# Retention outputs stored from POOL's queue, and adaLN products ordered behind a tile's decayed scores on VectorE

## The chip, the core and the metric

The kernel runs on one core of a Trainium2 chip. A core has TensorE (matrix products), VectorE, ScalarE, GpSimd (POOL) and SyncE (SP, which here only starts transfers), each with an instruction stream of its own that it takes in order, and 16 DMA engines. The metric is the device time of one launch in microseconds. Three runs of the kernel before gave 1794.5, 1806.36 and 1819.52 us, median 1806.36.

## What is computed

One layer of a diffusion backbone over 1024 tokens of width 1024, with 256 context tokens, all in float32: adaLN-modulated RMSNorm, one input projection split into differential attention and bidirectional retention, gates, output projection, then a mixture of 64 experts. The part that matters here is the retention output, and the adaLN vectors that are computed beside it:

```python
mod_x = jax.nn.silu(c) @ ada_w[l] + ada_b[l]
...
scores = jnp.einsum('bnihd,bnjhd->bnhij', qc, kc) * decay
intra = jnp.einsum('bnhij,bnjhe->bnihe', scores, vc)
...
cross = jnp.einsum('bnihd,nbhde->bnihe', q_dec, state_prev)
out = (intra + cross).reshape(b, t, h, dv)
...
r = jax.nn.silu(gate) * rmsnorm(ret, ret_norm_g).reshape(bn, t, R_V)
```

The forward and the backward direction are added; the kernel takes one two-sided decay matrix and both states stacked.

## The kernel before

The tokens are eight tiles of 128. The kernel goes in stages: adaLN columns and norm, then projections of the retention queries and keys, of the values with the chunk states (lines 503 to 534, ten tiles with the context), then the **retention loop** (lines 566 to 592), then the attention projections, attention, output projection, routing and experts.

The retention loop runs over t = 7 down to 0. In one iteration it transposes the queries and keys of the tile (line 392, `transpose4`), copies them (571, 574), calls `ret_out` for the tile before it, steps the backward state (`state_step`, lines 499 and 500), loads queries, keys and values of the next tile (`load_qkv`, lines 544 and 545, and the decayed queries, 547), projects the gate (24 matmuls of line 228), applies SiLU (582) and multiplies by the norm's weight on POOL (583, the gate product), computes the scores in PSUM (587) and multiplies them by the decay into sT (589, VectorE). `ret_out` multiplies sT with the values and the queries with the state (554, 555), squares the result with its sum (559), takes the reciprocal root (157 on VectorE, 159 a power on POOL), scales and gates it into r_o (563, four operations on VectorE) and stores r_o to `mix_d` in device memory (564, from SP's queue). What is stored there is read again by the output projection (line 874).

The remaining four adaLN vectors are 4096 columns, taken as 64 **products**: for each of 8 blocks of 512 columns and each of 8 slices of the input, 256 KB of weights are loaded (408, SP's queue, two buffers `ada_l`) and multiplied by a scalar per partition into an accumulator of 512 columns (410 for the first slice, 412 for the others, VectorE). `ada_rest(count)` emits `count` of them: three in each of the ten value tiles, and six (`GADA`) in each iteration of the retention loop, called behind sT, till none is left. After the third slice of a block `ada_row` closes the block before it: a matmul with ones sums over partitions (420), a bias row is added (424), and the row is stored.

Within an engine the order of instructions is not the order of the program text: a scheduler sets it when the program is built, by what is ready first in its own estimate, unless an order is asked for. A dependency of the kind NoSync between two instructions of one engine asks for that order and adds no semaphore.

Of the kernel before, what the change touches and what calls it, by code (L numbers as in the profile page):

```python
# [15 lines left out]
OP = mybir.AluOpType  # L16
# [4 lines left out]
P = 128  # L21
# [63 lines left out]
def hybrid_layer_kernel(ctx: ExitStack, tc: tile.TileContext, A, out, dbg=None):  # L85
    nc = tc.nc
    pe, dve, act, pool, sp = nc.tensor, nc.vector, nc.scalar, nc.gpsimd, nc.sync
# [58 lines left out]
    mix_d = dram.tile([SEQ, D], F32, name="mix_d")  # L146
# [7 lines left out]
    def rstd_cols(pl, ssq, n, width, scale):  # L154

        v = pl.tile([P, 8], F32, name="rs_v", tag="rs_v", bufs=4)
        dve.tensor_scalar(v[:n, :width], ssq, scale, EPS, op0=OP.mult, op1=OP.add)  # L157
        r = pl.tile([P, 8], F32, name="rs_r", tag="rs_r", bufs=4)
        pool.tensor_tensor(r[:n, :width], v[:n, :width], mhalf[:n].to_broadcast([n, width]), op=OP.pow)  # L159
        return r[:n, :width]  # L160
# [64 lines left out]
    def project(t, w, n0=0, n1=512):  # L225
        ps = psa.tile([P, 512], F32, name="pp", tag="pp", bufs=2)
        for kw in products(ps, t, w, n0, n1):
            pe.matmul(kw["out"], kw["lhsT"], kw["rhs"], start=kw["start"], stop=kw["stop"])  # L228
        return ps
# [28 lines left out]
    cc = consts.tile([P, KT, 2], F32, name="cc")  # L258
# [21 lines left out]
    for kind in range(2):  # L280
        for fb in range(2):
            dve.tensor_scalar(Wd[:, kind, :, fb], lg[:, 4 * fb:4 * fb + 4], pw[:, 2 * kind + fb:2 * kind + fb + 1],
                              None, op0=OP.mult)
# [105 lines left out]
    def transpose4(src, tag):  # L389
        pt = psa.tile([P, 4, P], F32, name="p4", tag=tag, bufs=2)  # L390
        for i in range(4):
            pe.transpose(pt[:, i, :], src[:, i * P:(i + 1) * P], ident)
        return pt
# [3 lines left out]
    VADA, GADA = 3, 6  # L397
    ada_acc = {}
    ada_left = [(n, k) for n in range(8) for k in range(KT)]

    def ada_rest(count):

        for n, k in ada_left[:count]:
            if k == 0:
                ada_acc[n] = wk.tile([P, 512], F32, name="ada_a", tag="ada_a", bufs=2)
            ac = ada_acc[n]
            aw = wk.tile([P, 512], F32, name="ada_l", tag="ada_l", bufs=2)
            sp.dma_start(aw, ada[:, k, 2048 + 512 * n:2560 + 512 * n])
            if k == 0:
                dve.tensor_scalar(ac, aw, cc[:, 0, 0:1], None, op0=OP.mult)  # L410
            else:
                dve.scalar_tensor_tensor(ac, aw, cc[:, k, 0:1], ac, op0=OP.mult, op1=OP.add)
            if k == 2 and n > 0:
                ada_row(n - 1)
        del ada_left[:count]

    def ada_row(n):
        c0 = 2048 + 512 * n
        pr_ = psa.tile([1, 512], F32, name="par", tag="po", bufs=2)
        pe.matmul(pr_, ones[:, 0:1], ada_acc.pop(n), start=True, stop=True)  # L420
        rw = wk.tile([1, 512], F32, name="ada_r", tag="ada_r")
        bw = wk.tile([1, 512], F32, name="ada_b", tag="ada_b")
        sp.dma_start(bw, A["ada_b"][:, c0:c0 + 512])
        dve.tensor_add(rw, pr_, bw)
        if n // 2 == 2:
            gw = wk.tile([1, 512], F32, name="ada_g", tag="ada_b")
            sp.dma_start(gw, A["norm2_g"][:, (n % 2) * 512:(n % 2 + 1) * 512])
            dve.scalar_tensor_tensor(rw, rw, 1.0, gw, op0=OP.add, op1=OP.mult)
        sp.dma_start(rows_d[n // 2:n // 2 + 1, (n % 2) * 512:(n % 2 + 1) * 512], rw)
# [15 lines left out]
    for i, g in enumerate(pairs):  # L445
        for t in (2 * g - 2, 2 * g - 1):
            if t < 0:
                ps = project(t, W, 256, 512)
                r = wk.tile([P, 256], F32, name="rkc", tag="rkc", bufs=2)
# [14 lines left out]
    Dm = wk.tile([P, H, P], F32, name="Dm")  # L464
# [31 lines left out]
    def state_step(dst, src, kvp, half):  # L496
        s = slice(64 * half, 64 * half + 64)
        tmp = wk.tile([P, H, P], F32, name="sst", tag="g2", bufs=NG2)
        dve.tensor_tensor(tmp[s], src[s], GSb[s], op=OP.mult)
        dve.tensor_add(dst[s], tmp[s], kvp[s])  # L500

    kvc0 = None
    for t in range(-2, NT):
        ada_rest(VADA)
        ps = project(t, W)
        v = wk.tile([P, 512], F32, name="rv", tag="g2", bufs=NG2)
# [35 lines left out]
    def load_qkv(t):  # L542
        qk, vt = rows_qv[:, t % 2, 0], rows_qv[:, t % 2, 1]
        sp.dma_start(qk, rqk_d[t * P:(t + 1) * P])
        sp.dma_start(vt, rv_d[t * P:(t + 1) * P])
        qd = wk.tile([P, H, 2, 64], F32, name="qd", tag="g2", bufs=NG2)
        dve.tensor_tensor(qd, qk[:, 0:256].rearrange("p (h d) -> p h d", h=H)[:, :, None, :].to_broadcast([P, H, 2, 64]),
                          Wd[:, 0, :, :, None].to_broadcast([P, H, 2, 64]), op=OP.mult)
        return qk, vt, qd

    def ret_out(t, sT, qdT, vt, gt):
        po_ = psa.tile([P, H, P], F32, name="po", tag="po", bufs=2)
        for h in range(H):
            pe.matmul(po_[:, h, :], sT[:, 2 * (h % 2) + h // 2, :], vt[:, h * P:(h + 1) * P], start=True, stop=False)
            pe.matmul(po_[:, h, :], qdT[:, h, :], ST[t][:, h, :], start=False, stop=True)
        ssq = wk.tile([P, 4], F32, name="ssq4", tag="ssq4", bufs=2)
        sqs = wk.tile([P, P], F32, name="sqs", tag="sqs", bufs=2)
        for h in range(H):
            act.activation(sqs, po_[:, h, :], AF.Square, accum_out=ssq[:, h:h + 1])
        rs = rstd_cols(wk, ssq, P, 4, 1.0 / P)  # L560
        r = wk.tile([P, H, P], F32, name="r_o", tag="g2", bufs=NG2)
        for h in range(H):
            dve.scalar_tensor_tensor(r[:, h, :], po_[:, h, :], rs[:, h:h + 1], gt[:, h, :], op0=OP.mult, op1=OP.mult)
        sp.dma_start(mix_d[t * P:(t + 1) * P, 512:1024], r.rearrange("p h e -> p (h e)"))

    nxt, out_args = load_qkv(NT - 1), None
    for t in reversed(range(NT)):
        qk, vt, qd = nxt
        pt = transpose4(qk, "tp")
        qkT = wk.tile([P, 4, P], F32, name="qkT", tag="g2", bufs=NG2)  # L570
        act.activation(qkT, pt, AF.Copy)
        pt = transpose4(qd.rearrange("p h a d -> p (h a d)"), "tp")
        qdT = wk.tile([P, H, P], F32, name="qdT", tag="g2", bufs=NG2)
        act.activation(qdT, pt, AF.Copy)
        if out_args:
            ret_out(*out_args)
        if t > 0:
            state_step(ST[t - 1], ST[t], ST[t - 1], 1)
            nxt = load_qkv(t - 1)
        ps = project(t, W)  # L580
        gt = wk.tile([P, H, P], F32, name="gt", tag="g2", bufs=NG2)
        act.activation(gt.rearrange("p h e -> p (h e)"), ps, AF.Silu)
        pool.tensor_tensor(gt, gt, rng[:, None, :].to_broadcast([P, H, P]), op=OP.mult)
        pss = psa.tile([P, 2, 4, P], F32, name="pss", tag="ps", bufs=1)
        for h in range(H):
            s = slice(64 * (h % 2), 64 * (h % 2) + 64)
            pe.matmul(pss[:, h % 2, h // 2, :], qkT[s, 2 + h // 2, :], qkT[s, h // 2, :], start=True, stop=True)
        sT = wk.tile([P, H, P], F32, name="sT", tag="g2", bufs=NG2)
        dve.tensor_tensor(sT.rearrange("p (a b) j -> p a b j", a=2), pss[:, :, 0:2, :], Dm.rearrange("p (a b) j -> p a b j", a=2), op=OP.mult)
        out_args = t, sT, qdT, vt, gt  # L590
        ada_rest(GADA)
    ret_out(*out_args)
    ada_row(NT - 1)

# [10 lines left out]
    for t in range(NT):  # L605
# [3 lines left out]
        for m in range(2):  # L609
            a, b = slice(64 * m, 64 * m + 64), slice(64 * (1 - m), 64 * (1 - m) + 64)  # L610
            act.activation(qs[a, m], pt[a], AF.Copy, scale=0.125)
            act.activation(qs[b, m], pt[a], AF.Copy, scale=0.125)
            for c in (a, b):
                dve.scalar_tensor_tensor(qs[c, 2 + m], pt[a], 0.125, qs[a, m].bitcast(F32), op0=OP.mult,
                                         op1=OP.subtract)
# [15 lines left out]
    for t in range(-2, NT):  # L631
# [8 lines left out]
        for m in range(2):  # L640
            a, b = slice(64 * m, 64 * m + 64), slice(64 * (1 - m), 64 * (1 - m) + 64)
# [662 lines left out]
    rest, order, lead = list(range(NEXP)), [], 0.0  # L1304
    while rest:
        r = rest.pop(0 if lead <= 0 else -1)
# [186 lines left out]
    with tc.For_i(0, n_over, 1) as j:  # L1493
        e = sp.value_load(olist[0:1, 0, bass.ds(j, 1)], min_val=0, max_val=NEXP - 1)
# [14 lines left out]
        for q in range(2):  # L1509
            pt = bank("tr", [P, 4, P])  # L1510
            for i in range(4):
                k = 4 * q + i
# [72 lines left out]
```

## Time and profile before

| what | us |
|---|---|
| median of three runs | 1806.36 |
| lowest, highest | 1794.5, 1819.52 |
| the profiled execution | 1810.34 |
| its span (first to last instruction) | 1808.5 |
| TensorE, VectorE, ScalarE, POOL busy | 1661.3, 1354.5, 960.8, 539.9 |

The profile is of one execution. It gives for each instruction its start, its length, its source line, and for idle time of an engine the event that ended it. In a name such as `ada_a<-ada_l,cc,ada_a` the output stands first and the inputs behind the arrow. PEld is TensorE's weight load, which overlaps the matmuls; SPq and POOLq are the instructions of those queues that start transfers. PEclk is the granted TensorE clock as a share of the full one. Matmuls are pipelined and their ends are modelled.

### The profile page before, as it was taken

How to read it: one execution, taken by the hardware profiler on the slowest of the kernel's cores; microseconds unless marked ns; L12 is line 12 of the kernel's file. 1: busy time of each engine (PE TensorE's matmuls, PEld its weight loads, DVE VectorE, ACT ScalarE, POOL GpSimd, SP SyncE). 2: the span in 40 equal slices, each digit the busy share in tenths (PEclk: the TensorE clock that was granted, in tenths of full speed). 3: DMA queues.
4: the chain of work that ended last, by engine and by line, in shares of the span. 5: the costliest groups of instructions: out<-in, count | busy, mean ns of one | idle time of the engine just before them, and what ended most of it. 6: DMA issues, size and time to landing. Idle time of an engine off the chain costs nothing.

```text
span 1808.5 us, 23059 instructions
## 1 busy us (share of the span) xinstructions
PE 1661.3 (92%) x8022; PEld 1264.4 (70%) x8022; DVE 1354.5 (75%) x2080; ACT 960.8 (53%) x1537; POOL 539.9 (30%) x384
## 2 busy tenths in 40 slices
PE   5899889999899989886999999999999999999992
PEld 3687677778566657665777777777776777777771
DVE  7866766642877757775678888888888988878873
ACT  6532333323577842131366686677675665566652
POOL 0100123200222130447335544333445333332331
PEclk9999999999899999998999999999999999999996
DMA  9675547601221154233989999999999999999976
GB/s 315 206 225 183 183 129 155 141 0 59 71 70 36 32 195 152 82 119 62 303 245 316 318 331 322 321 311 295 336 322 306 353 332 353 319 293 321 315 221 212
DMA packets 128413, 400.57 MB, mean 221 GB/s; under 512 B 13110, under 2 KB 49654, under 8 KB 103336
## 3 DMA queue, kind: packets, MB, share of 16 engines
q1 hardware_dynamic: 81000, 297.10, 45.8%
q0 software_dynamic: 46144, 97.80, 23.0%
q10 hardware_dynamic: 1152, 4.19, 0.6%
q8 instruction: 64, 1.05, 0.2%
q14 instruction: 53, 0.43, 0.1%
HBM read 324.45 MB, written 74.60 MB: 221 GB/s over the span
## 4 chain that ended last, share of the span: by engine, by line
PE 50%; DMA 18%; DVE 17%; ACT 7%; issue 5%; POOL 1%; SPq 1%; another core or an unknown queue 1%; POOLq 0%; DVEq 0%; ACTq 0%
PE up L1239 16%; DMA acc<-y,sidx 12%; PE py L1239 8%; PE pp L228 7%; PE py L97 3%; DVE w L1169 3%; PE pp L97 3%; PE tr L1223 3%; PE pS L97 3%; PE pu L97 2%; ACT w L1168 2%; DVE nmx L738 2%; DMA eraw<-in_exp_w_dram 1%; DMA ada_l<-in_ada_w_dram 1%; PE ptt L97 1%
## 5 line engine op out<-in xcount | busy, mean ns | idle before, releaser
L1239 PE MATMUL up<-w,xT 128*128 128x512 f32 (+1 forms) x2136 | 531.2, 398 | 6.4 <-DVE xT L1228 6.1
L1169 DVE TENSOR_TENSOR w<-eraw,w 128x1024 fp32r<-128x1024 f32 x390 | 459.7, 1217 | 44.1 <-ACT w L1168 43.3
L1168 ACT ACTIVATE w<-eraw 128x1024 fp32r<-128x1024 f32 x390 | 399.8, 1056 | 114.3 <-PE up L1239 60.7
L1239 PEld LDWEIGHTS up<-w,xT 128*128 128x128 f32 (+1 forms) x2136 | 382.7, 183 | 103.9 <-DVE xT L1228 10.2
L1178 POOL DMA_INDIRECT acc<-y,sidx x96 | 215.2, 2242 | 484.8 <-DMA acc<-y,sidx 158.9
L1239 PE MATMUL py<-w,ehT 128*128 128x512 f32 (+1 forms) x1116 | 293.4, 405 | 4.0 <-DVE ehT L1228 4.0
L1239 PEld LDWEIGHTS py<-w,ehT 128*128 128x128 f32 (+1 forms) x1116 | 198.2, 185 | 51.9 <-DVE ehT L1228 5.3
L1290 DVE SCALAR_TENSOR_TENSOR y<-py,swt,g2r 128x512 f32<-128x512 f32 (+2 forms) x192 | 137.8, 740 | 61.7 <-DMA acc<-y,sidx 39.0
L228 PE MATMUL pp<-whi,hTh 128*128 128x512 f32 (+1 forms) x368 | 146.5, 399 | 1.3 <-ACT hTh L386 1.2
L228 PE MATMUL pp<-wlo,hTh 128*128 128x512 f32 (+1 forms) x368 | 144.7, 394 | 0.0
L738 DVE TENSOR_REDUCE nmx<-pS 128x1 f32<-128x1280 f32 x64 | 95.1, 1487 | 65.8 <-PE pS L97 65.4
L1207 POOL DMA_INDIRECT xg<-h2tab,sidx x96 | 122.3, 1274 | 64.2 <-PE tr L1223 40.6
L1265 ACT ACTIVATE sl<-up 128x256 f32<-128x256 f32 (+1 forms) x104 | 39.7, 382 | 148.4 <-PE up L1239 136.4
L1228 DVE TENSOR_TENSOR xT<-tr,xT 128x512 fp32r<-128x512 f32 (+1 forms) x167 | 104.3, 654 | 17.0 <-ACT xT L1227 13.9
L1027 POOL DMA_INDIRECT slots<-dat,ad x64 | 68.7, 1073 | 109.8 <-DVE dat L1024 54.9
L159 POOL TENSOR_TENSOR rs_r<-rs_v,mhalf 128x1 f32<-128x1 f32 (+1 forms) x34 | 27.3, 802 | 244.3 <-DVE rs_v L157 146.8
L97 PE MATMUL pS<-K,qsl 128*128 128x512 f32 x336 | 95.7, 422 | 2.8 <-ACT an L746 1.9
L1227 ACT ACTIVATE xT<-tr 128x512 fp32r<-128x512 f32 (+1 forms) x167 | 89.1, 571 | 13.0 <-remote 4.4
L1223 PEld LDWEIGHTS tr<-cst,xg 128*128 128x128 f32 (+2 forms) x800 | 79.0, 140 | 22.3 <-issue 7.1
L1267 DVE TENSOR_TENSOR hn<-up,sl 128x256 f32<-128x256 f32 (+1 forms) x104 | 64.8, 623 | 39.3 <-ACT sl L1265 37.0
L97 PE MATMUL py<-wo,mT 128*128 128x512 f32 x384 | 90.7, 394 | 0.0
L1223 PE MATMUL tr<-cst,xg 128*128 128x128 f32 (+2 forms) x800 | 90.3, 253 | 0.1
(324 smaller groups left out, 2490.5 us busy)
## 6 DMA issues: line engine op xcount, KB each, us to landing
eraw<-in_exp_w_dram SPq DMA_DIRECT2D x192, 1024.0 KB
ada_l<-in_ada_w_dram SPq DMA_DIRECT2D x64, 256.0 KB
wraw<-in_w_in_dram SPq DMA_DIRECT2D x24, 512.0 KB
aw<-in_ada_w_dram SPq DMA_DIRECT2D x8, 1024.0 KB
qsp<-qs POOLq DMA_DIRECT2D x32, 256.0 KB
qsl<-qsp POOLq DMA_DIRECT2D x7, 1024.0 KB
xt<-in_x_dram SPq DMA_DIRECT2D x8, 512.0 KB
wor<-in_w_out_dram SPq DMA_DIRECT2D x8, 512.0 KB
```

The lines of the kernel that those rows point to most:

```text
L97: i = getattr(self.eng, name)(*args, **kw)
L228: pe.matmul(kw["out"], kw["lhsT"], kw["rhs"], start=kw["start"], stop=kw["stop"])
L738: dve.tensor_reduce(self.nmx, self.pS, axis=AX.X, op=OP.max, negate=True)
L1168: act.activation(hi, raw, AF.Copy)
L1169: dve.tensor_sub(lo, raw, hi.bitcast(F32))
L1178: x = pool.indirect_dma_start(out=acc, out_offset=bass.IndirectOffsetOnAxis(ap=idx, axis=0), in_=y, in_offset=None, compute_op=OP.add)
L1207: self.load = pool.indirect_dma_start(out=self.xg[:self.n], out_offset=None, in_=h2tab, in_offset=bass.IndirectOffsetOnAxis(ap=self.idx, a ...
L1223: pe.transpose(pt[:, i, :], src[:rows, k * P:(k + 1) * P], ident[:rows, :rows])
L1227: act.activation(hi, pt, AF.Copy)
L1228: dve.tensor_sub(lo, pt, hi.bitcast(F32))
L1239: pe.matmul(po, ops[o][:, k, :], w(k), start=(k == 0 and j == 0), stop=(k == nk - 1 and j == len(seq) - 1))
L1290: dve.scalar_tensor_tensor(y[:n, c], ps[i][:n], self.wt, g2r[:n, c], op0=OP.mult, op1=OP.mult)
```

## The change

The store of r_o is issued by POOL instead of SP. `ada_rest` gets an optional instruction `after`; when it is given, each product gets a NoSync dependency on it, so that it stands behind it in VectorE's order. The retention loop passes the instruction that writes sT. The loads of the products, the row sums and the calls in the value stage are as before.

```diff
@@ -398,7 +398,7 @@
-    def ada_rest(count):
+    def ada_rest(count, after=None):
@@ -407,9 +407,12 @@
             if k == 0:
-                dve.tensor_scalar(ac, aw, cc[:, 0, 0:1], None, op0=OP.mult)
+                x = dve.tensor_scalar(ac, aw, cc[:, 0, 0:1], None, op0=OP.mult)
             else:
-                dve.scalar_tensor_tensor(ac, aw, cc[:, k, 0:1], ac, op0=OP.mult, op1=OP.add)
+                x = dve.scalar_tensor_tensor(ac, aw, cc[:, k, 0:1], ac, op0=OP.mult, op1=OP.add)
+            if after is not None:
+                tc.add_manual_dep(x.ins, after.ins.name, mybir.DependencyInfo(
+                    mybir.DependencyClass.NoSync, mybir.DependencyReason.DATA), reason="issue order")
@@ -561,7 +564,7 @@
-        sp.dma_start(mix_d[t * P:(t + 1) * P, 512:1024], r.rearrange("p h e -> p (h e)"))
+        pool.dma_start(mix_d[t * P:(t + 1) * P, 512:1024], r.rearrange("p h e -> p (h e)"))
@@ -586,9 +589,9 @@
-        dve.tensor_tensor(sT.rearrange("p (a b) j -> p a b j", a=2), pss[:, :, 0:2, :], Dm.rearrange("p (a b) j -> p a b j", a=2), op=OP.mult)
+        decayed = dve.tensor_tensor(sT.rearrange("p (a b) j -> p a b j", a=2), pss[:, :, 0:2, :], Dm.rearrange("p (a b) j -> p a b j", a=2), op=OP.mult)
         out_args = t, sT, qdT, vt, gt
-        ada_rest(GADA)
+        ada_rest(GADA, decayed)
```

## Rows read from the trace of the kernel before

**Rows 1.** The page of the execution: its first line

```profile
span 1808.5 us, 23059 instructions
```

**Rows 2.** Busy time of each engine (instructions), granted clock, DMA share, GB/s, by stretch

```profile
core 0: us, PE busy (x) PEld busy (x) DVE busy (x) ACT busy (x) POOL busy (x), PEclk, DMA share, GB/s
188.50:201.00 12.50, 9.31 (x56) 7.59 (x56) 8.34 (x16) 3.29 (x12) 2.29 (x2) 1.00 0.55 178
201.00:213.50 12.50, 11.85 (x58) 9.12 (x58) 7.89 (x14) 2.44 (x10) 2.31 (x2) 0.86 0.51 159
...
225.40:238.10 12.70, 11.17 (x53) 8.76 (x54) 8.79 (x16) 2.07 (x9) 2.76 (x2) 0.87 0.47 150
...
250.70:259.80 9.10, 8.34 (x51) 6.94 (x52) 5.58 (x12) 2.07 (x9) 1.45 (x2) 1.00 0.37 116
```

**Rows 3.** Waits of 185 to 275 us: who for whom, us in total, times, longest

```profile
PEld po L554 <- DVE sT L589: 12.8, 8, 3.3
...
DVE ada_a L412 <- DMA ada_l<-in_ada_w_dram: 12.0, 11, 2.8
...
SPq L564 <- DVE r_o L563: 21.7, 7, 8.8
```

**Rows 4.** VectorE in order of time: start, us, line, operation [idle before, ended by]

```profile
200.91 0.69 DVE L589 TENSOR_TENSOR sT<-pss,Dm 128x512 f32<-128x512 f32 x1
203.08 0.75 DVE L412 SCALAR_TENSOR_TENSOR ada_a<-ada_l,cc,ada_a 128x512 f32<-128x512 f32 x1 [1.48 <-DMA ada_l<-in_ada_w_dram]
204.72 0.75 DVE L412 SCALAR_TENSOR_TENSOR ada_a<-ada_l,cc,ada_a 128x512 f32<-128x512 f32 x1 [0.89 <-DMA ada_l<-in_ada_w_dram]
206.36 0.17 DVE L157 TENSOR_SCALAR rs_v<-ssq 128x4 f32<-128x4 f32 x1 [0.89 <-ACT sqs L559]
207.72 1.13 DVE L563 SCALAR_TENSOR_TENSOR r_o<-po,rs_r,gt 128x128 f32<-128x128 f32 x4 [1.19 <-POOL rs_r L159]
...
210.32 0.69 DVE L500 TENSOR_TENSOR ST<-sst,ST 64x512 f32<-64x512 f32 x1
211.04 2.43 DVE L412 SCALAR_TENSOR_TENSOR ada_a<-ada_l,cc,ada_a 128x512 f32<-128x512 f32 x2
213.39 0.68 DVE L589 TENSOR_TENSOR sT<-pss,Dm 128x512 f32<-128x512 f32 x1
```

**Rows 5.** TensorE and POOL in order of time, same columns

```profile
210.84 0.71 PE L587 MATMUL pss<-qkT 64*128 64x128 f32 x8
211.48 1.02 PE L420 MATMUL par<-ada_a,ones 128*1 128x512 f32 x2
...
211.62 1.30 POOL L583 TENSOR_TENSOR gt<-gt,rng 128x512 f32<-128x512 f32 x1 [3.93 <-ACT gt L582]
...
259.36 1.57 POOL L583 TENSOR_TENSOR gt<-gt,rng 128x512 f32<-128x512 f32 x1 [2.89 <-ACT gt L582]
```

**Rows 6.** Groups by line, 187 to 275 us: busy us, mean ns, idle before

```profile
L412 DVE SCALAR_TENSOR_TENSOR ada_a<-ada_l,cc,ada_a 128x512 f32<-128x512 f32 x22 | 19.3, 879 | 12.4 <-DMA ada_l<-in_ada_w_dram 12.0
...
L410 DVE TENSOR_SCALAR ada_a<-ada_l,cc 128x512 f32<-128x512 f32 x3 | 2.4, 816 | 0.0
```

**Rows 7.** Chain of waits in order of time: start, us, what (slow and full clock)

```profile
203.01 0.43 PE po L554 x2
...
252.17 0.22 PE po L554 x2
```

**Rows 8.** Busy time by stretch, columns as in rows 2, behind the loop

```profile
275.00:300.00 25.00, 25.00 (x114) 19.98 (x113) 15.81 (x30) 6.92 (x12) 6.98 (x9) 1.00 0.56 111
```

**Rows 9.** Instructions of lines 589 and 617: ns min/median/max, first and last start

```profile
L589 DVE TENSOR_TENSOR sT<-pss,Dm x8: 678/684/693, 188.5 to 270.1; 128x512 f32<-128x512 f32 x8
...
L617 POOL DMA_DIRECT2D qsp<-qs x32: 708/892/1057, 287.8 to 339.0; - x32
```

**Rows 10.** SP's queue in order of time

```profile
208.87 0.33 SPq L564 DMA_DIRECT2D mix_d<-r_o  x1
211.82 0.33 SPq L408 DMA_DIRECT2D ada_l<-in_ada_w_dram  x1
```

## Prediction, written before the changed kernel was run

> **What bounds the kernel now.** I read the page first: the span is 1808.5 us [rows 1]; the execution profiled took 1810.3 us, 1.8 us around its span and 4 us above the median of the three runs, 1806.4. The change touches one stage, the retention loop (lines 567 to 592, eight tiles from t = 7 down to 0). I found its place by the decayed scores sT, one per tile: they start at 188.5, 201, 213.5, 225.4, 238.1, 250.7 and 259.8 us, and I asked for the busy time of each engine between those starts [rows 2]. The reader is to see that tiles with adaLN products cost 12.4 us each (five periods, 250.7 - 188.5 = 62.2 us) and the first without a full set 9.1 us.
>
> The waits inside the stage tell why [rows 3]. TensorE's weight loads wait for one thing, sT: eight times, 12.8 us. VectorE waits 12.0 us for the loads of adaLN rows. SP's queue waits 21.7 us for r_o, in front of its store. VectorE's own order [rows 4] shows how the first two hang together: behind sT stand two products that wait for their loads (203.08, 204.72), then rs_v, r_o and the three state and query operations (done at 211.01), then two more products that take 2.43 us, and only then the next sT at 213.39. Its scores had ended on TensorE at 210.84 + 0.71 = 211.55 [rows 5]. So sT is 1.8 us late by the products ahead of it, and TensorE, which has only eight transposes left to do, stands still.
>
> **The order of the products.** 64 products less 3 in each of ten projection tiles leaves 34 for this loop, six for each of t = 7 to 3 and four for t = 2. In the window from 187 us on there are 22 + 3 = 25 of them [rows 6], one of which ends just as the first sT starts. So 24 are done behind the first sT and 10 ahead of it. After the change none of the 34 may stand ahead of it, and those of tile t stand behind sT of t. That is a move of 10 x 0.75 = 7.5 us of VectorE work into the loop (0.75 us a product, [rows 4]).
>
> *Gain, upper bound.* If TensorE never waits for sT, 12.8 us go [rows 3]. In two periods the granted clock was 0.86 and 0.87, and a pair of output matmuls took 0.43 us instead of 0.22 [rows 2, 7]; eight pairs make 1.7 us more in each, and these dips followed TensorE's standing still. They may go too: 12.8 + 3.4 = 16 us. From the other side: the 9.1 us period, plus the adaLN row sum of 1.02 us [rows 5] that it lacks, is 10.1 us; five periods of 12.44 to 10.1 give 11.7, the first sT's wait 1.6 (12.8 / 8): 13.3. I keep 15 us as the end.
>
> *Gain, the value taken.* VectorE has six products to place per tile. Two can follow sT at once (loaded during the tile before) and are free: rs_v came 4.8 us behind the end of sT in a period of slow clock (206.36 - 201.60, [rows 4]), 3.1 us without the 1.7. The next two are loaded when those free their two buffers. A pair ends as the sT behind it begins (211.04 + 2.43 = 213.47 against 213.39); the products behind the sT of 200.91 came 2.1 us (203.08) and 3.7 us (204.72) after the end of the pair ahead of it, at about 201.0 [rows 4]. So the second pair arrives 1.5 + 2.1 = 3.6 and 1.5 + 3.7 = 5.2 us behind the end of sT, beside rs_v and the 1.2 us from rs_v's end to r_o (206.53 to 207.72) in which POOL takes the power; together they cost the chain 0.5 to 1.5 us. The last two arrive about when the next sT is due and are best behind it. So a period is 9.1 + 1.0 for products + about 0.5 of the row sum that isn't hidden = 10.6 us. Five periods: 5 x (12.44 - 10.6) = 9.2. The first sT comes 1.6 earlier. The last two periods, now with the tail of the 34 (four of t = 2 and the lag), get 0.9 each: -1.8. Sum: 9.0 us off. Behind the loop comes the query projection, in which TensorE is busy for 25.00 of 25 us [rows 8], so it starts as early as the loop ends and nothing there gives the gain back.
>
> *The two products that meet POOL.* The pair took 2.43 us where two alone take 1.5 because POOL's gate product (211.62 to 212.92) ran beside its second [rows 4, 5]. sT itself does not seem to mind: one gate product ran from 259.36 to 260.93 and thus over the whole sT of 259.8 [rows 5], and no sT took over 0.693 us [rows 9]. So behind the change the collision falls behind sT, under the output matmuls; this is inside the 9.0.
>
> **The store on POOL's queue.** SP's store waits 21.7 us, but what stands behind it? The store goes out at 208.87, the next load at 211.82, which is 0.03 us after the first product of the pair at 211.04 has ended (211.04 + 0.75) [rows 4, 10]. So the loads waited for their buffers and not for the store, and in the order of before the move alone is worth 0. In the order of after, loads are issued right behind sT, ahead of r_o, so the store could block only the third pair: worth 0 to 1 us a tile, and taken as part of the 10.6. On POOL an issue costs 0.71 to 1.06 us, by the query stores [rows 9]; it stands between the power and the next gate product, which needs to end only by the next r_o: this slack hides it. Nothing reads the stored rows before the output projection (line 874), so its landing costs nothing either. If that cover goes, it is 8 x 0.9 = 7 us. The same bytes move whichever queue starts them. The Trainium skill (DMA: Bandwidth & Descriptors, Issuing engines are not separate DMA queues) says that another issuing engine saves the time of the issue alone; the loads of rows 10, which did not wait for the store, agree, and by that rule this half would be worth next to nothing.
>
> **Rivals.**
>
> *Lock on VectorE (0 to 2 us off).* The store's issue work on POOL begins as r_o ends, just when VectorE does the state update and the query product. If those are held as the second product of the pair was (2.43 - 1.5 = 0.9 us, [rows 4]), then 8 x 0.9 = 7 us come back and next to nothing is won: 1805. Against it: that row was a POOL operation over 128x512 elements, not an issue; the trace has none beside such VectorE work here. The Trainium skill (SBUF — State Buffer, Who interferes with whom) has a rule that points this way, a port pair that VectorE and GpSimd lock for a whole instruction, though for a VectorE operation with two SBUF inputs it counts only GpSimd's reads. The trace's 2.43 agrees with the lock; none of its rows shows an issue against it.
>
> *The loads bound it (slower).* VectorE takes its queue in order. If more than about five products stand between two sT, the third pair is waited for. One pair, from the end of the pair before to its own end, takes 204.72 + 0.75 - 200.91 = 4.6 us [rows 4]; three make 13.7, plus sT 14.4 us a period: 5 x (14.4 - 12.44) = 9.8 slower, less 1.6 at the start: 8 us slower, 1814. It decides where all six of a tile stand ahead of the next sT. For it: 12.0 us are waited for loads already [rows 3], with 24 products, and 34 are to come. Against it: TensorE's scores are done early, and what is ready and traced first is not held back.
>
> *The change only moves the wait (none).* Six products (4.5), sT, the state and query operations (3 x 0.69), rs_v, four r_o (1.13) and 1 to 2 us of collisions are 9.5 to 10.5 us [rows 4] of VectorE per tile; with waits of 1.2 for POOL and 0.7 for late loads a period can come to 12.4 again: 1806.
>
> *All of it (15 off).* Every stall goes and the clock stays up: 1791.
>
> **How the numbers follow.** Chances: the 9 us gain 0.42, all of it 0.13, wait only moved 0.17, lock 0.10, slower by loads 0.18. Against the median of before, 1806.4, the likeliest is 1806.4 - 9 = 1797 (1801 against the profiled 1810.3); its own range is 1790 to 1804. The three runs of before lie 25 us apart, so a median can be off by some 6 to 8 us; with the cases from 1791 to 1814 the range is 1785 to 1815. About 2% (36 us) is what a measurement of this kernel can tell from no change. No case reaches it: faster 0.02, within 0.96, slower 0.02, the outer two for a change in the order of later stages that I can't see here.
>
> **What would show it.** Right: TensorE's wait for sT falls from 12.8 to under 4 us, the five periods to 10 to 11 us, no store of r_o on SP's queue, products right behind each sT. The granted clock stays at 1.00 in all periods if the dips were the stalls' doing. The loads' rival shows as VectorE waits for loads well above 12 us and periods of 13 and more; the lock as query products or state updates of over 1 us beside store issues. What would make the prediction wrong is a product waiting for its load ahead of rs_v or sT in most tiles, or an adaLN row sum that TensorE meets before its last product.

## The result, and the profile after

The change made the kernel slower: 1820.5 us against 1809.24 (medians of 19 runs each), a ratio of 1.0059 with a 95% interval of 1.0040 to 1.0079. That is within 2%, but on the other side of zero than forecast, and above the range of 1785 to 1815. The profiled execution has a span of 1815.6 us, 7.1 more than before [rows 1].

The forecast went by the distance from one sT to the next, so I read this first: busy time by stretch after the change, cut at the starts of sT (columns as in rows 2).

```profile
core 0: us, PE busy (x) PEld busy (x) DVE busy (x) ACT busy (x) POOL busy (x), PEclk, DMA share, GB/s
185.20:200.10 14.90, 11.64 (x68) 8.67 (x69) 10.77 (x17) 3.75 (x12) 4.39 (x4) 1.00 0.60 189
200.10:213.50 13.40, 11.39 (x55) 8.51 (x54) 9.22 (x16) 3.27 (x11) 3.31 (x3) 0.87 0.48 156
213.50:227.40 13.90, 11.71 (x62) 9.95 (x63) 9.98 (x18) 3.86 (x12) 3.29 (x3) 0.88 0.53 158
227.40:241.70 14.30, 11.74 (x65) 8.55 (x64) 10.38 (x18) 3.27 (x11) 3.27 (x3) 0.99 0.53 163
241.70:259.80 18.10, 15.67 (x76) 11.71 (x76) 10.68 (x18) 2.45 (x10) 2.90 (x3) 0.92 0.53 159
259.80:270.60 10.80, 9.78 (x58) 7.40 (x56) 7.90 (x13) 6.82 (x15) 2.90 (x3) 1.00 0.31 98
270.60:277.50 6.90, 5.93 (x37) 4.75 (x37) 5.32 (x11) 3.02 (x10) 2.12 (x2) 1.00 0.50 160
```

Five periods take 259.8 - 185.2 = 74.6 us, 14.9 each, where before took 12.44 [rows 2] and 10.6 was forecast. The first sT is 3.3 us earlier, the last 7.4 later (270.1 before, [rows 9]). The dips of the granted clock to 0.86 and 0.87 have not gone. The period of 18.1 us holds more work than one tile: TensorE ran the next tile's projection and scores (until 247.4) before the output matmuls (from 248.79) of the sT of 241.70, and the last two periods are shorter for that, 17.7 us together where before took 19.3.

The waits in the loop after the change (183 to 285 us, so that the last sT is in), for who waited for whom (us in total, times, longest):

```profile
PEld po L557 <- DVE sT L592: 3.2, 3, 1.4
PE p L392 <- DVE qd L550: 13.0, 6, 2.9
DVE ada_a L412 <- DMA ada_l<-in_ada_w_dram: 8.4, 8, 1.9
POOL mix_d L567 <- DVE r_o L566: 13.7, 6, 2.8
```

The wait that was to go has gone: TensorE's weight loads wait 3.2 us for sT, before 12.8 [rows 3]. In its place stands one of 13.0 us for qd, the decayed queries of the next tile (line 550 on VectorE), which TensorE transposes ahead of the output matmuls; before had no such wait. The store's 21.7 us on SP's queue [rows 3] have become 13.7 us on POOL. VectorE waits less for loads, 8.4 us against 12.0 [rows 3].

One tile of after, in order of time (VectorE, POOL and the transposes of qd):

```profile
219.63 0.17 DVE L157 TENSOR_SCALAR rs_v<-ssq 128x4 f32<-128x4 f32 x1 [2.60 <-ACT sqs L562]
219.71 0.75 DVE L412 SCALAR_TENSOR_TENSOR ada_a<-ada_l,cc,ada_a 128x512 f32<-128x512 f32 x1
221.40 0.35 DVE L566 SCALAR_TENSOR_TENSOR r_o<-po,rs_r,gt 128x128 f32<-128x128 f32 x1 [0.94 <-POOL rs_r L159]
221.66 0.74 DVE L412 SCALAR_TENSOR_TENSOR ada_a<-ada_l,cc,ada_a 128x512 f32<-128x512 f32 x1
222.32 0.86 DVE L566 SCALAR_TENSOR_TENSOR r_o<-po,rs_r,gt 128x128 f32<-128x128 f32 x3
222.97 0.60 ACT L585 ACTIVATE gt<-pp 128x512 f32<-128x512 f32 x1 [3.38 <-issue]
223.22 0.69 DVE L502 TENSOR_TENSOR sst<-ST,GS 64x512 f32<-64x512 f32 x1
223.48 0.60 POOL L567 DMA_DIRECT2D mix_d<-r_o  x1 [2.12 <-DVE r_o L566]
223.94 2.00 DVE L550 TENSOR_TENSOR qd<-rows_qv,Wd 128x512 f32<-128x512 f32 x1
224.11 1.28 POOL L586 TENSOR_TENSOR gt<-gt,rng 128x512 f32<-128x512 f32 x1
225.97 0.69 DVE L503 TENSOR_TENSOR ST<-sst,ST 64x512 f32<-64x512 f32 x1
226.09 0.63 PE L392 MATMUL p<-cst,qd 128*128 128x128 f32 x4 [1.96 <-DVE qd L550]
226.69 0.75 DVE L412 SCALAR_TENSOR_TENSOR ada_a<-ada_l,cc,ada_a 128x512 f32<-128x512 f32 x1
227.36 0.68 DVE L592 TENSOR_TENSOR sT<-pss,Dm 128x512 f32<-128x512 f32 x1
```

Two things are new here. A product (221.66) stands between the first r_o and the other three, in the chain r_o, state product, qd that TensorE waits for. And qd takes 2.00 us: POOL's gate product starts 0.17 us behind it and runs beside it. Before, the collision with the gate product fell on adaLN products [rows 4, 5] and state updates, and no qd took over 0.69 us. From the profile of before, a state update beside a gate product, and the lengths of all qd (ns min/median/max):

```profile
197.62 1.81 DVE L500 TENSOR_TENSOR ST<-sst,ST 64x512 f32<-64x512 f32 x1
...
L547 DVE TENSOR_TENSOR qd<-rows_qv,Wd x8: 686/693/693, 179.5 to 258.4; 128x512 f32<-128x512 f32 x8
```

### The profile page after: what moved, and what is told of

It is laid out like the page before. It is cut to its first block, busy times and chain, and to the rows that moved or that the text cites. A ratio compares the mean times of both kernels' runs of the same rounds, so it can differ in the third digit from the quotient of the medians.

```text
span 1815.6 us, 23066 instructions
## 1 busy us (share of the span) xinstructions
PE 1667.8 (92%) x8022; PEld 1267.4 (70%) x8022; DVE 1358.2 (75%) x2080; ACT 960.9 (53%) x1537; POOL 538.0 (30%) x392
## 4 chain that ended last, share of the span: by engine, by line
PE 44%; DMA 16%; DVE 13%; ACT 5%; issue 5%; POOL 1%; another core or an unknown queue 1%; SPq 0%; POOLq 0%; DVEq 0%; ACTq 0%
PE up L1242 16%; DMA acc<-y,sidx 11%; PE py L1242 7%; PE pp L228 4%; DVE w L1172 3%; PE pp L97 3%; PE py L97 3%; DMA eraw<-in_exp_w_dram 3%; PE pS L97 3%; PE tr L1226 3%; PE pu L97 2%; DVE nmx L741 2%; ACT w L1171 1%; PE ptt L97 1%; DVE y L1293 1%
## 5 line engine op out<-in xcount | busy, mean ns | idle before, releaser
L1181 POOL DMA_INDIRECT acc<-y,sidx x96 | 204.3, 2128 | 488.8 <-DMA acc<-y,sidx 170.6
L1210 POOL DMA_INDIRECT xg<-h2tab,sidx x96 | 127.8, 1331 | 65.4 <-PE tr L1226 41.7
L1230 ACT ACTIVATE xT<-tr 128x512 fp32r<-128x512 f32 (+1 forms) x167 | 89.1, 571 | 13.3 <-remote 7.6
```

The lines of the kernel that those rows point to most:

```text
L1181: x = pool.indirect_dma_start(out=acc, out_offset=bass.IndirectOffsetOnAxis(ap=idx, axis=0), in_=y, in_offset=None, compute_op=OP.add)
L1210: self.load = pool.indirect_dma_start(out=self.xg[:self.n], out_offset=None, in_=h2tab, in_offset=bass.IndirectOffsetOnAxis(ap=self.idx, a ...
L1230: act.activation(hi, pt, AF.Copy)
```

## The experiments

Two causes are possible for the loss: the order (products in the chain to qd) and the store on POOL (the gate product behind it lands on qd). The runs take them apart, then mend the order. The 95% intervals are about 0.5% wide; e1 to e4, e5 to e8 and e9 to e11 each share one chip and one set of runs of before. The landmarks are from the profiled execution of each. Identical kernels differ in the loop by up to 2.8 us (7 in where it ends), and from the attention on, where all kernels have one instruction order, spans differ by ten and more, so I compare positions only up to the first load of the output projection.

| kernel | median / before's | ratio, 95% | first, last sT | output projection from |
|---|---|---|---|---|
| before | 1809.24 | 1 | 188.5, 270.1 | 635.3 |
| after | 1820.5 / 1809.24 | 1.0059, 1.0040 to 1.0079 | 185.2, 277.5 | 643.6 |
| e1_store_only | 1803.85 / 1805.75 | 0.9995, 0.9965 to 1.0024 | 189.7, 272.0 | 637.5 |
| e2_order_only | 1804.97 / 1805.75 | 0.9979, 0.9955 to 1.0004 | 184.1, 270.0 | 632.3 |
| e3_gate_first | 1809.29 / 1805.75 | 1.0029, 1.0004 to 1.0054 | 183.7, 269.8 | 631.3 |
| e4_later | 1805.18 / 1805.75 | 1.0005, 0.9984 to 1.0027 | 185.1, 251.2 | 635.2 |
| e5_fence3 | 1792.57 / 1799.07 | 0.9972, 0.9945 to 0.9999 | 188.7, 261.9 | 632.2 |
| e6_fence4 | 1792.55 / 1799.07 | 0.9965, 0.9939 to 0.9991 | 184.8, 259.9 | 627.6 |
| e7_after_again | 1810.19 / 1799.07 | 1.0060, 1.0032 to 1.0088 | 186.5, 276.0 | 640.5 |
| e8_gate_first_again | 1801.2 / 1799.07 | 1.0013, 0.9987 to 1.0039 | 184.1, 272.5 | 637.0 |
| e9_order_only_again | 1799.76 / 1795.47 | 1.0014, 0.9990 to 1.0038 | 188.9, 277.0 | 639.7 |
| e10_fence4_pool | 1793.72 / 1795.47 | 0.9987, 0.9965 to 1.0010 | 184.5, 260.6 | 628.7 |
| e11_fence4_again | 1790.56 / 1795.47 | 0.9967, 0.9944 to 0.9991 | 184.3, 259.7 | 625.1 |

**The store alone.** Before, with one line changed:

```diff
-        sp.dma_start(mix_d[t * P:(t + 1) * P, 512:1024], r.rearrange("p h e -> p (h e)"))
+        pool.dma_start(mix_d[t * P:(t + 1) * P, 512:1024], r.rearrange("p h e -> p (h e)"))
```

> The kernel before with the store of r_o on POOL's queue alone; VectorE's and TensorE's orders stay those of before. Theory A (two causes: products ahead of the decayed queries, and the gate product pushed by the store onto the decayed queries): the gate product starts behind r_o and its store, the decayed queries take 2.0 us instead of 0.69, but the pair of products ahead of sT no longer meets it (1.5 instead of 2.43), so 0.4 us a tile are left: 0 to 4 us slower, ratio 1.000 to 1.002. Theory B (the store on POOL is the whole loss): 11 us slower, ratio 1.006. Theory C (the order alone): ratio 1.000.

Measured: 0.9995. In the order of before the store's issue is over before the gate's SiLU ends in all tiles but one, so the gate product starts when it did. In that one tile it meets qd (198.86, 2.24 us). The store by itself costs nothing that can be measured. Theory B is out. Theory A had the ratio nearly right and the mechanism wrong: it expected the collision with qd in every tile. Theory C's ratio fits; the next run is its test.

**The order alone.** After, with the store back on SP:

```diff
-        pool.dma_start(mix_d[t * P:(t + 1) * P, 512:1024], r.rearrange("p h e -> p (h e)"))
+        sp.dma_start(mix_d[t * P:(t + 1) * P, 512:1024], r.rearrange("p h e -> p (h e)"))
```

> The changed kernel with the store of r_o back on SP's queue; VectorE's order in the loop is that of the changed kernel. Theory A: the gate product runs when ScalarE has finished, ahead of the decayed queries, which take 0.69 us again; five times 1.3 us of the 11 go, 3 to 6 us slower than before, ratio about 1.0025, TensorE's wait for the decayed queries falls from 13 us to about 6. Theory B: no slower than before, ratio 0.995 to 1.000. Theory C: ratio 1.006, TensorE's wait for the decayed queries stays near 13 us.

> The order alone (store on SP) again, to narrow its interval. Theory A (order alone moves TensorE's wait from sT to the decayed queries and starts the loop earlier): loop end as before, ratio 0.996 to 1.001. If the order alone were the loss: 1.004 to 1.008.

Measured: 0.9979 and, on another chip, 1.0014: no change, and theory C (1.006) is out. Theory A had expected 1.0025 and a wait for qd of about 6 us, and for the repeat a loop that ends as before; that profile's last sT is 6.9 us later (277.0). The waits for qd and the lengths of qd in the first of the two profiles, then the lengths in the profile of after (min/median/max ns, first and last start):

```profile
PE p L392 <- DVE qd L550: 9.1, 6, 2.1
L550 DVE TENSOR_TENSOR qd<-rows_qv,Wd x8: 683/692/693, 177.4 to 260.7; 128x512 f32<-128x512 f32 x8
```

```profile
L550 DVE TENSOR_TENSOR qd<-rows_qv,Wd x8: 684/1346/2233, 178.5 to 268.1; 128x512 f32<-128x512 f32 x8
```

VectorE's order in the loop is that of after, and the new wait is there with no long qd: 9.1 us (9.2 in the repeat, where one qd took 1.65 us). So the order alone trades the wait for sT for one of nearly the same size; the first five periods are 13.6 us (252.3 - 184.1 = 68.2), in the repeat 14.3, against 12.44 before, the last two shorter. Together with the first run: neither half is a loss, the two together are 1.006. It is an interaction.

**The gate product ahead of the store.** After, with each store issued behind the next tile's gate product in POOL's order (`ret_out` returns the store as a function; a NoSync dependency asks for the order):

```diff
-        pool.tensor_tensor(gt, gt, rng[:, None, :].to_broadcast([P, H, P]), op=OP.mult)
+        gp = pool.tensor_tensor(gt, gt, rng[:, None, :].to_broadcast([P, H, P]), op=OP.mult)
+        if store:
+            tc.add_manual_dep(store().ins, gp.ins.name, mybir.DependencyInfo(
+                mybir.DependencyClass.NoSync, mybir.DependencyReason.DATA), reason="issue order")
```

> The changed kernel with each store of r_o ordered behind the gate product of the next tile on POOL; VectorE's and TensorE's orders in the loop are those of the changed kernel. Theory A: as with the store on SP, ratio about 1.0025, decayed queries at 0.69 us. If the store's issue itself holds VectorE: ratio stays at 1.006 though the gate product is early, and operations of VectorE beside the stores are long. Theory C: ratio 1.006.

> The changed kernel again, on the chip of the next one. Both theories: ratio 1.004 to 1.008; decayed queries of 2 us in four of the loop's tiles.

> The changed kernel with the stores behind the gate products on POOL, again, beside the changed kernel on one chip. If the collision of the gate product with the decayed queries is the loss: 5 to 8 us faster than the changed kernel (its loop is 6.2 us shorter in the profile), ratio to before 0.998 to 1.003. If something else of the store on POOL costs time: the same ratio as the changed kernel.

Measured: 1.0029 and 1.0013, the second on one chip with after's 1.0060: 1801.2 against 1810.19 us, and the fastest run of after there took 1801.95. The orders of VectorE and TensorE in the loop are the same; only POOL's differs, so most of the loss is that order. What it does shows where the gate product starts. After the change it starts 1.77, 0.42, 0.54, 2.56 and 4.30 us behind the end of its SiLU in five tiles in a row (the tile above: SiLU until 223.57, gate 224.11), because the store stands in front of it, waits for r_o (13.7 us in all) and is then issued. r_o, state product and qd follow one another on VectorE, so a gate product that the end of r_o releases lands on qd: four of them took 2.00 to 2.23 us (in the repeat three). In the kernel with the gate first, the same tile:

```profile
218.94 0.69 DVE L502 TENSOR_TENSOR sst<-ST,GS 64x512 f32<-64x512 f32 x1
219.66 1.64 DVE L550 TENSOR_TENSOR qd<-rows_qv,Wd 128x512 f32<-128x512 f32 x1
...
219.24 1.51 POOL L585 TENSOR_TENSOR gt<-gt,rng 128x512 f32<-128x512 f32 x1 [2.60 <-ACT gt L584]
220.70 0.60 POOL L567 DMA_DIRECT2D mix_d<-r_o  x1
```

This is the one tile in which it still meets qd; in the others it starts 0.08 us behind SiLU (0.9 where POOL is at the power) and meets other operations. TensorE's wait for qd is 9.3 and 9.0 us instead of 13.0 and 10.5, and the loop 86.1 and 88.4 us from first to last sT instead of 92.3 and 89.5.

Not all of this is POOL's order, for the granted clock differs too: order alone had 1.00 in all seven periods of its first profile, after had dips to 0.87, 0.88 and 0.92. Periods at a clock of 1.00: the first and the fourth of order alone, then the fourth of the repeat of after (columns as in rows 2):

```profile
184.10:198.10 14.00, 11.60 (x68) 8.63 (x69) 9.90 (x16) 3.76 (x12) 3.71 (x3) 1.00 0.64 196
221.40:235.20 13.80, 10.85 (x62) 7.76 (x61) 9.89 (x18) 3.24 (x11) 2.66 (x2) 1.00 0.52 153
...
226.20:240.50 14.30, 10.83 (x61) 7.74 (x61) 10.37 (x18) 3.27 (x11) 3.27 (x3) 1.00 0.52 152
```

So the first period is 14.9 (after) against 14.0, the fourth 14.3 against 13.8. The third is a test by itself: with qd stretched it took 13.87 us in after, at a clock of 0.88, against 13.48 in the repeat of order alone, at 0.87; in the repeat of after qd kept 0.69 us there, and the period was 11.56 us against 11.55 in order alone, both at 1.00. With the second (13.41 against 13.05, both at 0.87) and the fifth (17.74 against 17.08, both at 1.00), I estimate from these rows that the late gate product costs 2 to 3 us in the loop. The medians on one chip differ by 9. So the runs show POOL's order to be the cause, and the traces show where 2 to 3 us of it go.

The means of the repeats against order alone (1.0021 and 0.9997) leave room for some 0.2% that a store on POOL costs otherwise; the intervals overlap, and I leave that open.

**The products out of the loop.** Before, with 32 of the 34 products moved into the query projection behind it (four a tile, four load buffers), two left in the first tile:

```diff
-        ada_rest(GADA)
+        ada_rest(2 if t == NT - 1 else 0)
...
             pool.dma_start(qsp[h, :, :, t * P:(t + 1) * P], qs[:, :, h, :])
+        ada_rest(4)
+    ada_row(NT - 1)
```

> The kernel before with 32 of the 34 products of the retention loop moved into the query projection (four per tile, four load buffers); the store on SP. If the products are what makes the loop long: periods of 9 to 9.5 us in place of 12.4, the loop 14 to 17 us shorter; with a query projection that TensorE fills alone, the kernel gains 10 to 17 us, ratio 0.991 to 0.995. If the query projection has no room for 32 products and 8.4 MB of loads, the gain comes back there: ratio 0.997 to 1.003 with TensorE waiting in that stage.

Measured: 1.0005. The loop without products takes 66.1 us from first to last sT, 15.4 less than before; five periods are 9.1 us and TensorE waits for almost nothing. So the upper bound of the forecast, 15 us, was the right size. But the gain is given back behind the loop: its end is 18.8 us earlier than before, the last query store 6.1 (332.9, before 339.0 [rows 9]), the first attention scores 1.4 (455.9 and 457.3). The window of the query projection, of this kernel and then of before:

```profile
285.00:345.00 60.00, 48.08 (x196) 35.18 (x197) 48.47 (x76) 19.83 (x31) 19.08 (x26) 0.91 1.02 238
```

```profile
285.00:345.00 60.00, 57.78 (x264) 45.44 (x263) 40.88 (x65) 24.27 (x40) 25.09 (x34) 1.00 0.99 193
```

TensorE now stands still for 12 of 60 us, and 11.1 of them are one wait (us in total, times, longest):

```profile
PE pp L228 <- DVE rt L241: 11.1, 3, 6.5
```

This is for the rotary embedding of the queries (`rt`) on VectorE, in whose order products and the scaling of finished queries now stand ahead of it. VectorE itself waits for no adaLN load in this window. So the fault is that of the loop over again: filler work stands ahead of what TensorE needs next. No wait of TensorE in this window ends with a transfer, though the DMA engines' busy share was 0.99 there before already. Moved work cost as much there as in the loop; to gain, it must fit where nobody waits.

**A fence at the other end.** The same kernel shows such a place, VectorE's wait for the squares ahead of rs_v (us in total, times, longest), 3.9 us a tile:

```profile
DVE rs_v L157 <- ACT sqs L560: 27.4, 7, 5.0
```

So here the products stand behind sT *and* rs_v stands behind the last product of the tile (`behind` is the NoSync dependency, `last_ada` the last product), which leaves none between r_o and qd; four a tile instead of six (five in the first two, so all 34 stay in the loop), three load buffers, the store on SP:

```diff
-        dve.tensor_scalar(v[:n, :width], ssq, scale, EPS, op0=OP.mult, op1=OP.add)
+        x = dve.tensor_scalar(v[:n, :width], ssq, scale, EPS, op0=OP.mult, op1=OP.add)
+        if fence:
+            behind(x, fence)
...
-    VADA, GADA = 3, 6
+    VADA, GADA = 3, 4
...
-        rs = rstd_cols(wk, ssq, P, 4, 1.0 / P)
+        rs = rstd_cols(wk, ssq, P, 4, 1.0 / P, last_ada[0])
...
-        ada_rest(GADA)
+        ada_rest(GADA + (t > NT - 1 - 2), decayed)
```

> As the fenced kernel with three products, but four per tile and five in the first two, so that all 34 stay in the loop. The fourth load waits for the first product of its tile, so rs_v is held by about 1 us a tile: periods of 10.5 to 11.5 us, last sT 262 to 266 us, 4 to 8 us faster, ratio 0.995 to 0.998. If the loads bound it: periods of 12.5 and more, no gain.

> The kernel with four fenced products per tile and the store on SP again, beside the one with the store on POOL on one chip. Ratio to before 0.994 to 0.998.

Measured: 0.9965 and 0.9967, 6.5 and 4.9 us under before, as expected, and 1% under the change on one chip (1792.55 against 1810.19). Both intervals lie below 1. One tile of VectorE in this kernel:

```profile
208.69 0.69 DVE L600 TENSOR_TENSOR sT<-pss,Dm 128x512 f32<-128x512 f32 x1
209.30 0.78 DVE L418 TENSOR_SCALAR ada_a<-ada_l,cc 128x512 f32<-128x512 f32 x1
210.01 0.67 DVE L435 TENSOR_TENSOR ada_r<-par,ada_b 1x512 f32<-1x512 f32 x1
210.61 1.51 DVE L420 SCALAR_TENSOR_TENSOR ada_a<-ada_l,cc,ada_a 128x512 f32<-128x512 f32 x2
213.25 0.75 DVE L420 SCALAR_TENSOR_TENSOR ada_a<-ada_l,cc,ada_a 128x512 f32<-128x512 f32 x1 [1.13 <-DMA ada_l<-in_ada_w_dram]
213.92 0.67 DVE L439 SCALAR_TENSOR_TENSOR ada_r<-ada_r,ada_g 1x512 f32<-1x512 f32 x1
214.52 0.15 DVE L157 TENSOR_SCALAR rs_v<-ssq 128x4 f32<-128x4 f32 x1
215.85 1.13 DVE L574 SCALAR_TENSOR_TENSOR r_o<-po,rs_r,gt 128x128 f32<-128x128 f32 x4 [1.19 <-POOL rs_r L161]
217.01 0.69 DVE L510 TENSOR_TENSOR sst<-ST,GS 64x512 f32<-64x512 f32 x1
217.73 0.69 DVE L558 TENSOR_TENSOR qd<-rows_qv,Wd 128x512 f32<-128x512 f32 x1
218.46 1.71 DVE L511 TENSOR_TENSOR ST<-sst,ST 64x512 f32<-64x512 f32 x1
220.19 0.69 DVE L600 TENSOR_TENSOR sT<-pss,Dm 128x512 f32<-128x512 f32 x1
```

All products of the tile stand between sT and rs_v, r_o to qd is unbroken, and the gate product's collision (1.71) falls on the state update behind qd. TensorE's wait for qd:

```profile
PE p L394 <- DVE qd L558: 1.7, 1, 1.7
```

The five periods from 198.07 to 249.38 are 10.3 us; the one ahead of them, with five products, is 13.3, so that the first five, the measure used above, come to 11.0. From first to last sT it is 75.1 us, before 81.5; the loop ends 10 us earlier than before, and in the two profiles the output projection starts 8 and 10 us earlier.

**Fewer products, same fence.** Three a tile in the loop (four in the first two) and the other eight in the query projection:

```diff
-    VADA, GADA = 3, 4
+    VADA, GADA = 3, 3
...
             pool.dma_start(qsp[h, :, :, t * P:(t + 1) * P], qs[:, :, h, :])
+        ada_rest(1)
+    ada_row(NT - 1)
```

> The changed kernel's idea fenced on both sides: three products per tile (26 of the 34 in the loop, the last 8 one per tile in the query projection), behind sT of the tile and ahead of its rs_v, so that none can stand ahead of the decayed queries; three load buffers instead of two; the store on SP. Theory A (the loss is that products stand between r_o and the decayed queries, and that the gate product is pushed onto these): TensorE waits neither for sT nor for the decayed queries, periods of 9.5 to 10.5 us, the last sT 12 to 16 us earlier than before (255 to 258 us), kernel 6 to 14 us faster, ratio 0.992 to 0.997. Rival (VectorE simply has too much to do with the products wherever they stand): periods stay above 12 us, ratio 0.998 to 1.002.

Measured: 0.9972, the same as four a tile. That is just past the end of theory A's range, and A's landmarks were missed: the last sT came 8.2 us earlier than before, not 12 to 16, and only some periods (9.1 to 12.5) fell under 10.5. The loop is 2 us shorter than with four a tile (73.2 against 75.1), and the output projection does not start earlier for it.

**The fence with the store on POOL.** The four-a-tile kernel with the one line of the first experiment:

> The kernel with four fenced products per tile and the store of r_o on POOL, ahead of the next gate product as in the changed kernel; VectorE's and TensorE's orders in the loop are those of the fenced kernel. Theory A (the store costs only where the gate product is ready before r_o and then falls on the decayed queries): here ScalarE's gate is done after r_o, so the store delays nothing, the decayed queries stay at 0.69 us in all but one tile, ratio to before 0.995 to 0.998 as with the store on SP. Rival (a store on POOL costs 0.6 to 0.8 us a tile wherever it stands): 5 to 7 us slower than the fenced kernel, ratio 0.999 to 1.001.

Measured: 0.9987 against 0.9967 of the same kernel with SP's store on that chip, 1793.72 and 1790.56 us; the intervals overlap, and 0.9987 lies between the ranges of the two theories, so this run decides for neither. Only one gate product met a qd (195.35, 2.23 us). With the chain to qd short, the store's issue ends before SiLU does in the other tiles, as in e1. That part of theory A held; whether the store costs some 0.2% otherwise stays open here too.

## Why the prediction was wrong

**What held.** The bound was read rightly: TensorE waited for sT because of products ahead of it, the change took that wait from 12.8 to 3.2 us (under 4 was forecast), and the products do not hold up sT. The loop without them shows that some 15 us were there. The rival of the loads did not happen: the periods of 13 and more came, but VectorE's wait for loads fell. The sentence of the Trainium skill (DMA: Bandwidth & Descriptors, Issuing engines are not separate DMA queues) that another issuing engine saves the time of the issue alone fits the store's own move (0.9995).

**First failed step: "The last two arrive about when the next sT is due and are best behind it".** The sum for 10.6 us ended each tile's chain at sT. The output matmuls also need the transposed decayed queries, and qd stands on VectorE behind r_o and the state product. The dependency asked for puts products behind one sT; it does not keep them from the other end, and those that come late stand in the r_o group and ahead of qd. The period came to 14.9 us with the store on POOL (14.3 in the repeat) and to 13.6 and 14.3 with it on SP, in place of 10.6. The size was nearly attainable: with a fence at both ends, and the products spread over all tiles, the same five periods are 11.0 and the loop 75.1 us, where the forecast's own terms make 81.5 - 9.2 + 1.8 = 74.1. The kernel then gained 5 to 6.5 us, not 9. The rival "only moves the wait" had the right outcome for this half (0.9979, 1.0014) though it looked for the new wait at VectorE's fullness, not at qd.

**Second failed step: "this slack hides it" for the store on POOL.** I counted the issue (0.58 to 0.80 us measured, 0.71 to 1.06 taken) and asked by when the gate product must end. I did not ask what stands behind the store while it *waits*: on SP that was a load with no free buffer, on POOL it is the gate product, held up by 0.42 to 4.30 us in five tiles. Nor did I ask what the gate product would then run beside. It had the slack; qd, which it stretched, had none. In the four tiles qd lost 1.54 + 3 x 1.31 = 5.5 us, of which up to 3.9 (13.0 - 9.1) show as TensorE's longer wait for it than with the store on SP; in the repeat three tiles lost 4.2, of which 1.3 (10.5 - 9.2) show.

**The lock's rival** had the right kind of collision and place, but the wrong partner. State products beside the store's issue kept 0.69 us, and so did qd where no gate product followed at once (in e1 the qd of 212.72, beside the issue of 212.28 to 212.89); the gate product that follows did the damage.

**Tail and clock.** The last two periods came out 1.7 us shorter (17.7 against 19.3), not 1.8 longer: the work of 18.1 us took part of theirs. The clock's dips to 0.87 stayed. That they were the stalls' doing is not borne out: order alone waited 9.1 us for qd with a clock of 1.00 in all periods, and its repeat, with the same waits, had two periods at 0.87. The kernel without products in the loop, which hardly waits there, kept 1.00 too, but what brings on a dip stays open.

**The range.** Its upper end, 1815, took in the loads' loss of 8 us, but not the lost cover of the store, priced at 7: the two halves were never priced together. That 1814 + 7 = 1821 is near the measured 1820.5 is luck, for the loads' loss did not happen; the interaction of the order with the store did.

**What stays open.** Measured, after costs 11 us. The late gate product is worth an estimated 2 to 3 us in the loop. The rest I could not place. The landmarks do not place it: after's last sT is 7.4 and 5.9 us late in its two profiles and its output projection 8.3 and 5.2, but the repeat of order alone is as late (6.9 and 4.4) with a ratio of 1.0014. In the runs on one chip the mean granted clock of after was 0.973 and that with the gate product first 0.975, so part of the rest may be the clock; no run takes that apart.

## What to carry to other kernels

An order that is asked for needs both ends: naming what the filler work stands behind does not say what it must stay ahead of, and the next thing that the bounding engine needs from that queue pays. When a transfer moves to another queue, price not its issue but its wait, and look up what stands behind it on the new queue and beside whose work that will then run. Two halves that are each free can lose together, so a change with two parts wants a price for the pair.

## What the runs showed of the hardware

Where a POOL operation over 128x512 elements stretched a VectorE operation with two inputs in SBUF (qd, state update, adaLN product of line 412), that operation ended about 0.55 us behind POOL's: qd of 223.94 ended at 225.94 and the gate product at 225.39; with the gate first 221.30 and 220.75; the state update above 220.17 and 219.61. The product of a block's first slice (410), which reads one tile in SBUF and a scalar per partition and takes 0.47 to 0.49 us alone, took 1.77 and ended 0.29 us behind (211.47 and 211.18). Operations that read PSUM were not stretched: four r_o took 1.12 us inside the gate product of 276.40, sT 0.69 inside that of 259.36 before [rows 5, 9]. The Trainium skill (SBUF — State Buffer, Who interferes with whom) says that a VectorE instruction with two SBUF inputs contends with a GpSimd instruction that reads SBUF; the 2.00 us of qd agree. It also says that issue order decides who blocks. The starts that the profile records do not always bear that out. In nine of the ten cases of after and its repeat in which the gate product directly followed the store on POOL, it kept 1.27 to 1.29 us and the operation that had started 0.17 to 0.40 us *earlier* was stretched, to 1.77 to 2.23 us; in the tenth the operation kept its 0.69 us and the gate product took 1.66. Where ScalarE released the gate product, an operation that had started 0.12 or 0.33 us earlier kept its time (before, 236.04, 0.75 us; the fenced kernel, 207.97, 0.69) and the gate product took 1.76 and 1.50. The two sets differ in what precedes the gate product; why, no run here tells.
